# Output projection of a hybrid diffusion block: weight sums from the other tile pool, x reloaded inside the stage, and the seven products reordered

## The chip, the cores and the metric

The kernel runs on one core of a Trainium2 chip. The metric is the device time of one execution in microseconds (us). The median of three executions of the kernel before the change is 942.68 us (942.07 to 944.18).

## The reference, cut to what matters

One layer of a token mixer with a convolutional feed-forward part, for 512 tokens of width 1024, plus 256 context tokens that only give two start states. All data are float32.

```python
hx  = rms_norm(x) * (1 + sc1x) + sh1x            # sh, sc, g: silu(c) @ w_ada + b_ada
u, vs, q, r, ga, gb, k, v, lr = split(hx @ w_in)
a   = gelu(u) * spatial_gate(gelu(vs))
ob  = gated_linear_attention(q, k, v, lr) * silu(r)
merged = sigmoid(ga) * (a @ w_br_a) + sigmoid(gb) * (ob @ w_br_b)
x   = x + g1x * (merged @ w_o)                   # the output projection: w_o is 1024 x 1024
h2  = rms_norm(x) * (1 + sc2x) + sh2x
aa, val = split(h2 @ w_up)                       # 1024 -> 2 x 2816
x   = x + g2x * ((gelu(conv3x3(aa)) * val) @ w_down)
out = rms_norm(x)
```

## The kernel before

Tokens lie in tiles of 128 partitions for the residual stream (four token tiles `t`, each in two column halves `hf` of 512: `x1[t][hf]`), and transposed, feature on partition, as input of a matmul. Every float32 operand is split into a high and a low part (`wh`, `wl` for a weight, `mh`, `ml` for the merged activations, `h2h`, `h2l` for the second norm's output), and each product is done in three passes, high x high, high x low, low x high.

**The weight stream.** Weights come in blocks of 512 KB (two row groups of 128 by 512 columns). A list `loads` issues each block on SyncE's DMA queue into a tile `raw` (four buffers); a list `specs` splits it, ScalarE casting to `wh` (line L138), VectorE subtracting to get `wl` (L139). `weights(lead, ahead)` gives the next block to the matmuls, splits `lead` further ones and issues loads `ahead` of it.

**The output projection** is `strassen()`: the 1024 x 1024 by 1024 x 512 product done as seven half-size products instead of eight. A product `prod` has two weight blocks `j`, and for each of them two token halves by two row groups by three passes, which makes 24 matmuls of 128x512 (L443). The stages ga, gb and r of `w_in` use the same routine just before. `w_strassen` makes their weights: b11, b12, b21, b22 are the four quarters of the weight matrix. Some products want sums of quarters. They are built in four tiles `tt` (128x512 each, two for each `j`): b22 is loaded by SyncE (L199), b12 is added by a DMA with accumulation that GpSimd issues (L186, `add_rows`), this sum is split (L207 on ScalarE, L208 on VectorE; `t` in the list), then b11 is added by VectorE (L218; split as `t2`), and then b21 by a second accumulating DMA (split as `t4`). For `w_o` alone the sum b12 + b11 is made by an accumulating DMA into b12's raw tile (L192). In the order of their weights the seven products are a11, s3, s2, a12, s1, a22, s4. The left letter's accumulators are PSUM tiles `mm` and `gl`; ScalarE copies one into another where two products share a start (L452, L457, L461).

**After a product** is complete `wo_done` multiplies it by the gate g1 (L1447), adds it into `x1` (L1448) and has ScalarE sum the squares (L1449). When a token tile has both column halves, `norm2_tok` scales it (`xs`, L1422, after a reciprocal root, L479 and L480), and when two token tiles have it, `norm2_half` transposes them on the matmul engine (L1434, 16 matmuls of 128x128), ScalarE applies scale and shift (`h2f`, L1439), and VectorE splits the result into `h2h` and `h2l` (L1442, L1443). Tokens 256 to 511 are half 1, tokens 0 to 255 half 0. The feed-forward part starts with four groups of matmuls on 256 tokens of half 1 (L381, 96 matmuls of 128x256), then the same four for half 0 (L370), and from then on all 512 tokens.

**Around it.** `ada` work on the side computes the modulation vectors for later stages: weights `wa` are loaded into `late` tiles, VectorE accumulates them into `acc` (L1138), the sums are split (`acch`, `accl`; ScalarE L362, VectorE L363) and summed over partitions by two matmuls each (L1144, L1145).

**Pools and queues.** Two pools of 2 KB-per-partition tiles serve almost everything: `heap` with 44 slots and `late` with 27. A load into a reused slot waits for the last reader of the old tile. `tt`, the splits of `acc`, `xs` and `h2f` come from `heap`; `x1`, `br`, `os`, `wa` and `acc` come from `late`. Each engine works through its instructions in one fixed order, and SyncE's and GpSimd's DMA issues also stand in one order each, so an issue that waits holds those behind it. The order is made when the program is built, by a scheduler that goes by the order of the code, the dependencies and when slots come free; `tc.add_manual_dep` forces one instruction behind another.

## Time and profile before

| what | value |
|---|---|
| median of 3 executions | 942.68 us (942.07 to 944.18) |
| the profiled execution | 942.39 us, of which 940.7 us are the span from first to last instruction |
| TensorE (PE) busy | 908.0 us, 97% of the span |
| VectorE (DVE) busy | 761.5 us, 81% |
| ScalarE (ACT) busy | 477.6 us, 51% |
| GpSimd (POOL) busy | 62.1 us, 7% |
| mean granted TensorE clock | 0.986 |

Times in the views are microseconds from the span's start. A row of the timeline gives start, duration, engine, line, operation, output <- input, sizes, count, and in square brackets how long the engine was idle before it and what released it. A row of the table by stretches gives busy time and count for PE, PE's weight loads, DVE, ACT and POOL, the granted clock, the share of DMA capacity and GB/s. Matmuls overlap, so the time of one is read from start to start.

### The profile page before, as it was taken

How to read it: one execution, taken by the hardware profiler on the slowest of the kernel's cores; microseconds unless marked ns; L12 is line 12 of the kernel's file. 1: busy time of each engine (PE TensorE's matmuls, PEld its weight loads, DVE VectorE, ACT ScalarE, POOL GpSimd, SP SyncE). 2: the span in 40 equal slices, each digit the busy share in tenths (PEclk: the TensorE clock that was granted, in tenths of full speed). 3: DMA queues.
4: the chain of work that ended last, by engine and by line, in shares of the span. 5: the costliest groups of instructions: out<-in, count | busy, mean ns of one | idle time of the engine just before them, and what ended most of it. 6: DMA issues, size and time to landing. Idle time of an engine off the chain costs nothing.

```text
span 940.7 us, 12862 instructions
## 1 busy us (share of the span) xinstructions
PE 908.0 (97%) x4671; PEld 759.8 (81%) x4671; DVE 761.5 (81%) x1328; ACT 477.6 (51%) x855; POOL 62.1 (7%) x90
## 2 busy tenths in 40 slices
PE   6999999999999999999999798999999999999996
PEld 5776898988888888888888677988888888888885
DVE  5567759688589877877776779699999998999797
ACT  5136546557465547566552366434333333466574
POOL 3000000000000011112001010000000000122100
PEclk9999999999999999999999989999999999999998
DMA  9941411131079375988545275244444333499532
GB/s 274 331 127 26 132 46 46 46 112 52 17 243 328 106 186 123 288 260 205 178 136 125 57 167 157 66 124 135 125 118 129 111 113 96 106 244 240 135 108 90
DMA packets 125821, 134.27 MB, mean 143 GB/s; under 512 B 7178, under 2 KB 84310, under 8 KB 125758
## 3 DMA queue, kind: packets, MB, share of 16 engines
q1 hardware_dynamic: 115357, 116.80, 39.8%
q0 software_dynamic: 8672, 15.43, 9.9%
q10 hardware_dynamic: 1728, 1.22, 0.4%
q8 instruction: 37, 0.61, 0.3%
q14 instruction: 27, 0.21, 0.1%
HBM read 131.32 MB, written 2.10 MB: 142 GB/s over the span
## 4 chain that ended last, share of the span: by engine, by line
PE 57%; DVE 30%; issue 5%; ACT 4%; DMA 4%; ACTq 0%; SPq 0%; DVEq 0%; POOL 0%; POOLq 0%
PE mm L370 9%; DVE cacc L1484 9%; PE gl L443 7%; PE mm L396 6%; DVE wl L139 6%; PE gl L1586 6%; PE mm L443 5%; PE mm L1586 4%; PE gl L396 3%; PE gl L885 3%; PE mm L389 2%; DVE acc L1138 2%; PE mm L675 2%; ACT wh L138 1%; PE mm L381 1%
## 5 line engine op out<-in xcount | busy, mean ns | idle before, releaser
L138 ACT CAST wh<-raw 128x1024 fp32r<-128x1024 f32 x110 | 115.0, 1049 | 115.8 <-PE mm L370 70.3
L139 DVE TENSOR_TENSOR wl<-raw,wh 128x1024 fp32r<-128x1024 f32 x110 | 133.7, 1218 | 36.9 <-ACT wh L138 36.5
L370 PE MATMUL mm<-h2l,wh 128*128 128x512 f32 (+1 forms) x352 | 133.6, 379 | 0.0
L370 PE MATMUL mm<-h2h,wh 128*128 128x512 f32 (+1 forms) x352 | 133.6, 379 | 0.0
L370 PE MATMUL mm<-h2h,wl 128*128 128x512 f32 (+1 forms) x352 | 133.5, 379 | 0.0
L1484 DVE SCALAR_TENSOR_TENSOR cacc<-ca,ccol,cacc 128x441 f32<-128x441 f32 (+2 forms) x176 | 121.5, 693 | 3.5
L370 PEld LDWEIGHTS mm<-h2h,wh 128*128 128x128 f32 x352 | 66.2, 188 | 12.6
L370 PEld LDWEIGHTS mm<-h2h,wl 128*128 128x128 f32 x352 | 66.2, 188 | 12.5
L370 PEld LDWEIGHTS mm<-h2l,wh 128*128 128x128 f32 x352 | 66.2, 188 | 12.3
L1485 ACT ACTIVATE cacc<-cacc 128x512 f32<-128x512 f32 x22 | 13.9, 633 | 72.6 <-DVE cacc L1484 72.5
L1138 DVE SCALAR_TENSOR_TENSOR acc<-wa,cs,acc 128x512 f32<-128x512 f32 x64 | 46.0, 746 | 4.4 <-DMA wa<-in_w_ada_dram 3.8
L207 ACT CAST wh<-tt 128x512 fp32r<-128x512 f32 x48 | 28.0, 620 | 27.8 <-DMA tt<-in_w_in_dram 8.9
L370 PE MATMUL mm<-hxh,wh 128*128 128x512 f32 x104 | 41.7, 401 | 0.0
L370 PE MATMUL mm<-hxh,wl 128*128 128x512 f32 x104 | 41.0, 394 | 0.0
L370 PE MATMUL mm<-hxl,wh 128*128 128x512 f32 x104 | 40.7, 392 | 0.0
L208 DVE TENSOR_TENSOR wl<-tt,wh 128x512 fp32r<-128x512 f32 x48 | 31.1, 684 | 8.9 <-ACT wh L207 8.8
L1528 ACT CAST wh<-raw 128x1024 fp32r<-128x1024 f32 x22 | 23.0, 1052 | 18.2 <-DVE raw L1539 8.1
L186 POOL DMA_DIRECT2D tt<-in_w_in_dram x24 | 20.8, 1044 | 166.8 <-DVE xl L1237 72.2
L1529 DVE TENSOR_TENSOR wl<-raw,wh 128x1024 fp32r<-128x1024 f32 x22 | 26.8, 1216 | 4.4 <-ACT wh L1528 4.3
L443 PE MATMUL mm<-wh,hxh 128*128 128x512 f32 x72 | 28.0, 389 | 0.0
L443 PE MATMUL mm<-wl,hxh 128*128 128x512 f32 x72 | 28.0, 389 | 0.0
L443 PE MATMUL mm<-wh,hxl 128*128 128x512 f32 x72 | 28.0, 389 | 0.0
(521 smaller groups left out, 2394.9 us busy)
## 6 DMA issues: line engine op xcount, KB each, us to landing
raw<-in_w_in_dram SPq DMA_DIRECT2D x54, 512.0 KB, 5.0
wa<-in_w_ada_dram SPq DMA_DIRECT2D x96, 256.0 KB, 5.9
raw<-in_ffn_w_up_dram SPq DMA_DIRECT2D x44, 512.0 KB, 3.8
raw<-in_ffn_w_down_dram SPq DMA_DIRECT2D x22, 512.0 KB, 3.4
tt<-in_w_in_dram POOLq DMA_DIRECT2D x24, 256.0 KB, 7.5
raw<-in_w_br_a_dram SPq DMA_DIRECT2D x8, 512.0 KB, 4.7
raw<-in_w_br_b_dram SPq DMA_DIRECT2D x8, 512.0 KB
raw<-in_w_o_dram SPq DMA_DIRECT2D x8, 512.0 KB, 4.5
```

What stands on the lines that cost most here:

```text
L138: A.copy(wh, raw)
L139: V.tensor_tensor(wl, raw, wh.bitcast(F32), op=ALU.subtract)
L207: A.copy(wh[:, kk, :], tt[j][kk])
L208: V.tensor_tensor(wl[:, kk, :], tt[j][kk], wh[:, kk, :].bitcast(F32), op=ALU.subtract)
L370: T.matmul(ps, a[:, k, :], b[:, c0:c0 + n], start=(k == 0 and i == 0), stop=(k == KT - 1 and i == 2))
L396: T.matmul(ps, a, b[:, k % 2, :], start=(k == 0 and i == 0), stop=(k == KT - 1 and i == 2))
L443: T.matmul(ps[t], a, b[:, kk, :], start=(first and i == 0), stop=(j == 1 and kk == 1 and i == 2), skip_group_check=again)
L885: T.matmul(ps, p_, q_, start=(start and z == 0), stop=(stop and z == 2))
L1138: V.scalar_tensor_tensor(a_, w_, cs[:, k, 0:1], a_, op0=ALU.mult, op1=ALU.add)
L1484: V.scalar_tensor_tensor(o, a_[:, r0 + dy:r1 + dy, c0 + dx:c1 + dx], wcol(tap), o, op0=ALU.mult, op1=ALU.add)
L1529: V.tensor_tensor(wl, raw, wh.bitcast(F32), op=ALU.subtract)
L1586: T.matmul(ps, a[:, t * P:(t + 1) * P], w[b][:, j, c0:c0 + n], start=(first and i == 0), stop=(last and i == 2), skip_group_check=again)
```

## The change

Four things are changed, all but the last for `w_o` alone.

1. The tiles `tt` of `w_o` come from `late` instead of `heap`.
2. The eight loads of x into `x1` (256 KB each) are no longer issued ahead of the stages (L1410) but inside the output projection's first step, behind the last load of b12 (`behind`).
3. `low_first`: the weights come in the order b11, t, t2, b12, t4, b21, b22, and the products in the order a11, s3, s2, s1, a22, a12, s4. The loads of b21 and b22 move back in the list to match. Half 1 of the tokens is now complete after a22 with two products (a12 and s4) still to come; before, with one (s4).
4. The high and low parts of the `ada2` sums come from `late` instead of `heap`.

```diff
+    def behind(start, name):
+        for i in traced()[start:]:
+            tc.add_manual_dep(i, name, mybir.DependencyInfo(
+                mybir.DependencyClass.NoSync, mybir.DependencyReason.DATA), reason="behind")
...
-                tt[j] = [heap([P, 512], s="tt") for _ in range(2)]
+                tt[j] = [(late if low_first else heap)([P, 512], s="tt") for _ in range(2)]
...
         specs.extend([split_b11(j) for j in js] + [(lambda j=j: split_t(j)) for j in js] + [split_t2(j) for j in js] +
-                     [split_raw("b21", j) for j in js] + [split_raw("b12", j) for j in js] +
-                     [(lambda j=j: split_t(j)) for j in js] + [split_raw("b22", j) for j in js])
+                     (t1 + t4 + b21 if low_first else b21 + t1 + t4) + [split_raw("b22", j) for j in js])
...
-                      (4, [load_b12(j) for j in js]), (6, [load_raw("b21", 1, 0, j) for j in js]),
-                      (10, [load_raw("b22", 1, 1, j) for j in js])):
+                      (4, [load_b12(j) for j in js]),
+                      (10 if low_first else 6, [load_raw("b21", 1, 0, j) for j in js]),
+                      (12 if low_first else 10, [load_raw("b22", 1, 1, j) for j in js])):
...
-    w_strassen(w_o[0], 0, True)
+    w_strassen(w_o[0], 0, True, True)
...
-        prod(a, "a12", True)
-        for t in range(2):
-            done(0, t, a[t], 1.0)
+
+        def c11():
+            prod(a, "a12", True)
+            for t in range(2):
+                done(0, t, a[t], 1.0)
+
+        if not low_first:
+            c11()
         prod(c, "s1", True)
...
         prod(b, "a22", True)
         for t in range(2):
             done(0, 2 + t, b[t], 1.0)
+        if low_first:
+            c11()
         prod(c, "s4", True)
...
-            ah, al = split_act(a_, s="acc", eng=A.copy)
+            ah, al = split_act(a_, s="acc", eng=A.copy, lo_pool=late, hi_pool=late)
...
+    def x1_load():
+        start = len(traced())
...
+        behind(start, last_load["b12"])
...
-    strassen(lambda name, k, t: [z[:, k * P:(k + 1) * P] for z in mg[name, t]], wo_done, do)
+    def wo_step():
+        if not x1:
+            x1_load()
+        do()
+
+    strassen(lambda name, k, t: [z[:, k * P:(k + 1) * P] for z in mg[name, t]], wo_done, wo_step, True)
```

The order of the program on each engine moves at four places. In the rows, the last number of a name is the buffer's own number, and the new program's lines are shifted (L181 is L186, L199 is L205, L207 is L213, L443 is L451, L1434 is L1454, L222 is L228, L363 is L371).

On SyncE's queue before, in the output projection: raw 5182 and 5184 are b11 (j 0 and 1), 5478 and 5481 are b12, 5484 and 5508 are b21; `tt` 5190 and 5191 belong to j 0, 5466 and 5467 to j 1.

```order
L181 DMA raw_1071_5182<-in_w_o_dram 128x2x512
L181 DMA raw_1072_5184<-in_w_o_dram 128x2x512
L181 DMA raw_1157_5478<-in_w_o_dram 128x2x512
L199 DMA tt_1075_5190<-in_w_o_dram 128x512
L199 DMA tt_1076_5191<-in_w_o_dram 128x512
L181 DMA raw_1158_5481<-in_w_o_dram 128x2x512
L181 DMA raw_1159_5484<-in_w_o_dram 128x2x512
L199 DMA tt_1153_5466<-in_w_o_dram 128x512
L199 DMA tt_1154_5467<-in_w_o_dram 128x512
```

On the same queue now, far ahead, in the stage of gb (the `raw` tiles are quarters of `w_in`; `tt` 5450 and 5451 are j 1 of `w_o`; `tt` 4515 belongs to the stage of r):

```order
L186 DMA raw_919_4381<-in_w_in_dram 128x2x512
L205 DMA tt_1075_5190<-in_w_o_dram 128x512
L186 DMA raw_923_4402<-in_w_in_dram 128x2x512
L205 DMA tt_1076_5191<-in_w_o_dram 128x512
L205 DMA tt_1145_5450<-in_w_o_dram 128x512
L186 DMA raw_937_4475<-in_w_in_dram 128x2x512
L186 DMA raw_940_4493<-in_w_in_dram 128x2x512
L205 DMA tt_1146_5451<-in_w_o_dram 128x512
L205 DMA tt_943_4515<-in_w_in_dram 128x512
```

All four `tt` loads of `w_o` left the place behind the wait for a free raw tile, and stand 19 to 25 issues ahead of b11; on GpSimd's queue their four adds stand directly ahead of the four first adds of the stage of r. Where they were, the queue now has b11, b12, the eight loads of x, b21, b22.

On the matmul engine before, at the end of the projection (s4's last matmuls, then the transposes of half 1):

```order
L443 MATMUL gl_1180_5607<-wl_1196_5703,mh_1121_5414 128x512
L443 MATMUL gl_1180_5607<-wh_1195_5702,ml_1122_5415 128x512
L1434 MATMUL gl_1211_5764<-ident_76,xs_1204_5747 128x128
L1434 MATMUL gl_1213_5776<-ident_76,xs_1204_5747 128x128
L1434 MATMUL gl_1215_5788<-ident_76,xs_1205_5748 128x128
```

The same engine now (wh 5676 is the first of s4's two weight blocks):

```order
L451 MATMUL gl_1178_5605<-wh_1190_5676,mh_1121_5414 128x512
L1454 MATMUL gl_1203_5720<-ident_76,xs_1196_5703 128x128
L1454 MATMUL gl_1205_5732<-ident_76,xs_1196_5703 128x128
L451 MATMUL gl_1178_5605<-wl_1191_5677,mh_1121_5414 128x512
L451 MATMUL gl_1178_5605<-wh_1190_5676,ml_1122_5415 128x512
L1454 MATMUL gl_1203_5720<-ident_76,xs_1201_5716 128x128
```

The transposes of half 1 moved from behind s4 into its middle, after the tenth of its 24 matmuls.

On ScalarE before, around the copies L461 that give s1 and s4 their start value (the raw tiles cast are b12 + b11):

```order
L461 COPY gl_1179_5606<-gl_1163_5522 128x512
L138 CAST wh_1181_5612<-raw_1158_5481 128x1024
L461 COPY gl_1180_5607<-gl_1164_5523 128x512
L207 CAST wh_1183_5628<-tt_1075_5190 128x512
L207 CAST wh_1183_5628<-tt_1076_5191 128x512
```

ScalarE now (the same copies are L469; the casts of `tt` 5190 and 5191 here are `t4`, that is, after b21's add):

```order
L143 CAST wh_1171_5566<-raw_1150_5465 128x1024
L213 CAST wh_1174_5584<-tt_1075_5190 128x512
L213 CAST wh_1174_5584<-tt_1076_5191 128x512
L469 COPY gl_1177_5604<-gl_1161_5518 128x512
L469 COPY gl_1178_5605<-gl_1162_5519 128x512
```

The two casts that wait for b21's accumulating DMA now stand ahead of the copies, and s1, the next product, starts from those copies.

On VectorE before, much earlier, in the last quarter of branch a (L222 are the sums of two quarters for the stage of ga, accl 3741 the low part of an `ada2` sum):

```order
L1234 TENSOR_TENSOR hxl_141_525<-hv_782_3719,hxh_140_524 128x256
L363 TENSOR_TENSOR accl_786_3741<-acc_631_3047,acch_785_3740 128x512
L222 TENSOR_TENSOR raw_811_3829<-raw_811_3829,raw_777_3696 128x1024
L222 TENSOR_TENSOR raw_824_3887<-raw_824_3887,raw_778_3698 128x1024
L139 TENSOR_TENSOR wl_823_3884<-raw_777_3696,wh_822_3883 128x1024
```

VectorE now:

```order
L1249 TENSOR_TENSOR hxl_141_525<-hv_782_3719,hxh_140_524 128x256
L228 TENSOR_TENSOR raw_811_3829<-raw_811_3829,raw_777_3696 128x1024
L228 TENSOR_TENSOR raw_824_3887<-raw_824_3887,raw_778_3698 128x1024
L371 TENSOR_TENSOR accl_786_3741<-acc_631_3047,acch_785_3740 128x512
L144 TENSOR_TENSOR wl_823_3884<-raw_777_3696,wh_822_3883 128x1024
```

The low part of the `ada2` sum moved behind the two sums that wait for loads of `w_in`. SyncE's queue there has a `tt` load of the stage of ga (256 KB) put between the two raw loads 3829 and 3887.

More of the change, by code (lines that the diff above doesn't have):

```diff
@@ L128, in backbone_kernel @@
     xin = tok_load(x[0], 4, heap)
-    specs, loads = [], []
+    specs, loads, last_load = [], [], {}
     def raw_tile(kn, n):
@@ L169, in w_wide, with w_strassen @@
                 w_cols(w, hf * 512, 512, 2 * k, 2, scaled)
-    def w_strassen(w, c0, add_b12=False):
+    def w_strassen(w, c0, add_b12=False, low_first=False):
         base = len(specs)
@@ L181, in load @@
                 dma(raws[name, j], blk(kh, nh, j).rearrange("(k p) c -> p k c", p=P))
+                last_load[name] = traced()[-1].name
             return load
@@ L233, in w_strassen @@
         js = range(2)
+        b21, t1 = [split_raw("b21", j) for j in js], [split_raw("b12", j) for j in js]
+        t4 = [lambda j=j: split_t(j) for j in js]
         specs.extend([split_b11(j) for j in js] + [(lambda j=j: split_t(j)) for j in js] + [split_t2(j) for j in js] +
-                     [split_raw("b21", j) for j in js] + [split_raw("b12", j) for j in js] +
-                     [(lambda j=j: split_t(j)) for j in js] + [split_raw("b22", j) for j in js])
+                     (t1 + t4 + b21 if low_first else b21 + t1 + t4) + [split_raw("b22", j) for j in js])
         for o, fs in ((0, [load_raw("b11", 0, 0, j) for j in js]), (2, [load_t(j) for j in js]),
-                      (4, [load_b12(j) for j in js]), (6, [load_raw("b21", 1, 0, j) for j in js]),
-                      (10, [load_raw("b22", 1, 1, j) for j in js])):
+                      (4, [load_b12(j) for j in js]),
+                      (10 if low_first else 6, [load_raw("b21", 1, 0, j) for j in js]),
+                      (12 if low_first else 10, [load_raw("b22", 1, 1, j) for j in js])):
             loads.extend((base + o + j, fs[j]) for j in js)
@@ L431, in wide_kk, with strassen @@
         wide_half(1, [gl() for _ in range(4)], acts, done, step, 2, 6)
-    def strassen(acts, done, step):
+    def strassen(acts, done, step, low_first=False):
         def prod(ps, name, again):
@@ L1405, in backbone_kernel @@
     x1 = []
-    for t in range(4):
-        row = []
-        for hf in range(2):
-            t_ = late([P, 512], s="x1")
-            dma(t_, x[0, t * P:(t + 1) * P, hf * 512:(hf + 1) * 512])
-            row.append(t_)
-        x1.append(row)
+    def x1_load():
+        start = len(traced())
+        for t in range(4):
+            row = []
+            for hf in range(2):
+                t_ = late([P, 512], s="x1")
+                dma(t_, x[0, t * P:(t + 1) * P, hf * 512:(hf + 1) * 512])
+                row.append(t_)
+            x1.append(row)
+        behind(start, last_load["b12"])
     ss2 = const([P, 4, 2], "ss2")
```

## The prediction

> **What bounds the kernel now.** I read the table by stretches first, to see in which stage the matmul engine (PE) is not full, then the timeline of that stage on all engines, then PE's alone.
>
> ```profile
> 526.00:534.70 8.70, 8.70 (x42) 7.01 (x40) 8.21 (x14) 3.83 (x7) 0.00 (x0) 1.00 0.09 25
> 534.70:542.20 7.50, 0.25 (x2) 0.05 (x1) 1.58 (x4) 1.34 (x3) 1.78 (x2) 0.80 0.71 172
> 542.20:549.00 6.80, 6.50 (x13) 4.13 (x14) 5.50 (x8) 4.17 (x8) 2.54 (x3) 0.50 0.51 80
> 549.00:576.50 27.50, 27.45 (x120) 22.34 (x119) 23.04 (x32) 17.61 (x29) 1.86 (x3) 0.99 0.71 194
> 576.50:580.50 4.00, 0.83 (x4) 0.40 (x4) 4.00 (x12) 2.88 (x7) 0.00 (x0) 0.96 0.80 237
> 580.50:583.40 2.90, 2.88 (x14) 2.89 (x15) 2.90 (x11) 2.53 (x8) 0.00 (x0) 0.50 0.16 42
> 583.40:596.60 13.20, 13.20 (x112) 13.20 (x112) 10.04 (x33) 5.90 (x13) 0.00 (x0) 0.99 0.14 39
> 596.60:800.00 203.40, 203.40 (x945) 170.40 (x944) 182.64 (x264) 75.31 (x98) 0.00 (x0) 1.00 0.39 118
> ```
>
> The second number is PE's busy time, the fourth VectorE's, the third from the end PE's clock. From 596.6 to 800 PE is full, so whatever arrives earlier at 596.6 shortens the run by as much. Two holes lie ahead: 534.7 to 549 (idle, then half clock) and 576.5 to 583.4.
>
> ```profile
> 531.15 0.68 DVE L1370 TENSOR_TENSOR mf<-mf,mf 128x512 f32<-128x512 f32 x1
> 531.76 0.68 DVE L218 TENSOR_TENSOR tt<-tt,raw 128x512 f32<-128x512 f32 x1
> ...
> 532.50 0.38 SPq L181 DMA_DIRECT2D raw<-in_w_o_dram  x1
> ...
> 533.00 0.87 SPq L199 DMA_DIRECT2D tt<-in_w_o_dram  x2
> ...
> 537.38 1.78 POOL L186 DMA_DIRECT2D tt<-in_w_o_dram  x2 [29.06 <-DMA tt<-in_w_o_dram]
> 541.48 1.14 ACT L207 CAST wh<-tt 128x512 fp32r<-128x512 f32 x2 [5.32 <-DMA tt<-in_w_o_dram]
> ```
>
> This is the first hole's cause. SyncE's next raw load, b21, needs the raw tile that the add L218 reads, so it goes out at 532.50, and only then the tt tiles of j 1 at 533.00. They land, GpSimd adds b12 (537.38), that lands 4.1 us later, ScalarE casts at 541.48, and the second half of s3 can start.
>
> ```profile
> 525.96 0.48 PE L443 MATMUL mm<-wh,mh 128*128 128x512 f32 x1
> ...
> 534.51 0.39 PE L443 MATMUL mm<-wh,ml 128*128 128x512 f32 x1
> 542.15 0.79 PE L443 MATMUL mm<-wh,mh 128*128 128x512 f32 x1 [7.25 <-ACT wh L207]
> ...
> 549.53 0.39 PE L443 MATMUL gl<-wh,ml 128*128 128x512 f32 x1
> ...
> 576.06 0.39 PE L443 MATMUL gl<-wh,ml 128*128 128x512 f32 x1
> 578.40 0.83 PE L1434 MATMUL gl<-ident,xs 128*128 128x128 f32 x4 [1.95 <-DVE xs L1422]
> 580.51 2.82 PE L1434 MATMUL gl<-ident,xs 128*128 128x128 f32 x12 [1.28 <-DVE xs L1422]
> ...
> 590.03 1.47 PE L1434 MATMUL gl<-ident,xs 128*128 128x128 f32 x12
> 591.25 0.36 PE L381 MATMUL mm<-h2l,wh 128*128 128x256 f32 x1
> ...
> 596.48 0.28 PE L381 MATMUL mm<-h2h,wl 128*128 128x256 f32 x1
> 596.60 0.28 PE L370 MATMUL mm<-h2h,wh 128*128 128x256 f32 x1
> ```
>
> Between 549.53 and 576.06 lie 117 starts, so a 128x512 matmul costs 26.53/117 = 0.227 us; one of 128x256 costs 0.12 (596.60 − 596.48), a transpose 0.10 (12 from 590.03 to 591.25). Of the projection's 168 matmuls 36 have run when the idle begins (534.51 + 0.23 = 534.74); the other 132 are worth 29.9 and take until 576.3, 41.6 later: 11.7 lost, of it 7.25 idle and most of the rest half clock until about 549. The second hole is VectorE's: from 576.5 to 583.4 it is busy throughout, because the last product's outputs, their residual adds and the scaling `xs` stand in a row, and PE has nothing left but the transposes that wait for them.
>
> **The ceiling.** With no stall, from 525.96: the first 36 as they were, 8.8; 132 more, 29.9; 32 transposes of both halves, 3.3; 96 × 0.12 = 11.5; in all 53.5. First L370 at 579.5 instead of 596.6: at most 17.1.
>
> **The change, part by part.**
>
> *tt from the other pool.*
>
> ```profile
> 522.81 1.23 DVE L139 TENSOR_TENSOR wl<-raw,wh 128x1024 fp32r<-128x1024 f32 x1
> 523.95 0.69 DVE L1348 SCALAR_TENSOR_TENSOR ml<-mf,mh 128x512 fp32r<-128x512 f32 x1
> ```
>
> The four tt loads are issued in the stage of gb, some 100 us ahead, and their b12 adds soon behind them. What SyncE holds back until 532.50 is then not on s3's path. s3's second half needs VectorE's `wl` of the last tt at 534.74. Following VectorE's new row order from the L139 at 522.81, with 0.61 for a 128x512 operation (531.76 − 531.15) and 1.14 for 128x1024 (523.95 − 522.81), it ends at about 532.4. So the idle and the half clock behind it go: 11.7.
>
> *What is late next.* (a) The second half of s2 needs `wl` of t2 at 541.1 and gets it at 541.3: nothing. (b) On ScalarE the casts of t4 stand ahead of the copies from which s1 starts. They wait for b21's adds, issued when VectorE has split t2 (534.8 and 537.2) and landing 4.1 or somewhat more later: 541.3 to 543. Then a cast and a copy, 0.5 to 0.6 each: s1 starts at 543.6 instead of 542.9. I take 0.7; from 0 to 2.
>
> *Products reordered.* Half 1 is complete after a22, with 48 matmuls (10.9 us) left instead of 24 (5.4). Its chain (outputs multiplied, added, squared, root, `xs`) now runs beside a12. VectorE has little room: from 526.00 to 596.60 its work is 8.21 + 1.58 + 5.50 + 23.04 + 4.00 + 2.90 + 10.04 = 55.3, against PE's 53.5, so the two are level and VectorE sets the pace. By its new order `xs` of half 1 comes at 562.8 to 564.2; the first transpose stands behind s4's tenth matmul, at 562.2. That leaves two stalls, 0.7 and 0.6, and the hole at s4's end goes, because the first L381 finds its input. (c) For half 0, VectorE finishes the last split at about 583.5 while L370 begins to ask at 582; from 0 to 1.5, I take 1.0.
>
> First L370: 579.5 + 0.7 + 1.3 + 1.0 = 582.5 instead of 596.6, a gain of 14.1.
>
> *x reloaded late.*
>
> ```profile
> 498.49 34.39 SPq L181 DMA_DIRECT2D raw<-in_w_o_dram  x2
> ```
>
> The eight loads of 256 KB leave the stages of gb and r, where PE was full with them, and are issued behind b12's last load, the first of these two issues, after which SyncE had nothing to send for over 30 us. They are needed after s1, at about 550. Nothing either way. The adds of b12 + b11 (L192) are as before.
>
> *acc splits in the other pool, and what their slots move.* At 341 us:
>
> ```profile
> 334.21 0.38 SPq L181 DMA_DIRECT2D raw<-in_w_in_dram  x1
> ...
> 334.77 0.69 DVE L363 TENSOR_TENSOR accl<-acc,acch 128x512 fp32r<-128x512 f32 x1
> ...
> 339.40 1.23 DVE L222 TENSOR_TENSOR raw<-raw,raw 128x1024 f32<-128x1024 f32 x1 [1.57 <-DMA raw<-in_w_in_dram]
> ...
> 341.68 0.68 DVE L363 TENSOR_TENSOR accl<-acc,acch 128x512 fp32r<-128x512 f32 x1
> 341.70 0.39 PE L1145 MATMUL mm<-accl,ones_r 128*128 128x512 f32 x1
> ```
>
> The first accl was made at 334.77, long before 341.70 where PE reads it. Now it stands behind the second L222, which waited for the raw load issued at 334.21 and landed at 339.4 (5.2 us for 512 KB). Ready: 339.4 + 1.14 + 0.6 = 341.2, just in time; but a tt load of 256 KB now stands ahead of that raw, worth up to half of those 5.2. If the landing slips by 1.0, PE waits 0.5. The second accl, ready at 342.3 before, now follows two splits and three small operations: about 0.8 more. PE has no idle there, so a stall counts in full. I take 1.3; from 0 (the loads overlap) to 2.6.
>
> Sum: 14.1 − 1.3 = 12.8. Against the profiled execution's own 942.39 (0.29 under the median of 942.68) that is 929.6.
>
> **The clock.** My sum has no clock term, since the new stalls are a third of those before 578.40 and 580.51. Those two, 1.95 and 1.28 with 0.83 of work between, were followed by 2.9 us at half clock (the row 580.50), so short gaps can cost; the rival below has that. The Trainium skill (TensorE: Matmul & The Clock Gate, "What's actually happening") has the half rate come after an idle window of about 3.4 us; by that rule neither those gaps nor the new ones would cost anything, and the trace disagrees where two follow one another.
>
> **The rivals.**
>
> *VectorE's row stalls on the accumulating DMAs* (0.13). If b21's adds land later than 543, the t4 splits and all behind them on VectorE slip, and at 55.3 of work there is no slack to make it up. Against it: 4.1 us from issue to use at 537.38. For it: four adds in 6 us, while x and b21 also load. 4.5 more would give first L370 at 587: 934.
>
> *The clock drops in s4* (0.10). If the stalls before the transposes count as those of 578.40 and 580.51, some 3 to 6 us at half clock follow, 1.5 to 3 lost: 931 to 932.6.
>
> *The change doesn't do what it says* (0.02): tt is late for another reason than the queue. Against it stand 532.50 and 533.00, back to back. Then only the second hole goes: 929.6 + 11.7 = 941.3.
>
> *Slower, by one queue* (0.03). On GpSimd the four adds of w_o stand ahead of the first adds of the stage of r, and the last of them waits for a tt load that SyncE issues only behind two raw loads.
>
> ```profile
> 425.71 1.76 POOL L186 DMA_DIRECT2D tt<-in_w_in_dram  x2 [14.97 <-DMA tt<-in_w_in_dram]
> ...
> 435.80 1.29 DVE L208 TENSOR_TENSOR wl<-tt,wh 128x512 fp32r<-128x512 f32 x2
> ...
> 436.26 0.39 PE L443 MATMUL mm<-wh,hxh 128*128 128x512 f32 x1
> ```
>
> r's s3, which uses that split, begins 24 × 0.227 = 5.4 after r's first matmul at 436.26, at 441.7, so the split done at 437.1 has 4.6 to spare. The delay I see is one landing and one issue, 1 to 2.5: hidden. To end slower it would have to exceed 4.6 + 12.8 = 17.4.
>
> **How the numbers follow.** My forecast, 927 to 932 for the sum with its ends, has 0.68; 0.04 lies below 927, where the stalls I count don't occur (floor 942.4 − 17.1 = 925.3). Measurement of this kernel can tell 0.2%, 1.9 us, from no change. Faster by more has 0.68 + 0.04 + 0.13 + 0.10 = 0.95, which I put at 0.94 for what I have not seen; same 0.03, the case of 941.3 and mixtures; slower 0.03. The range 926.0 to 934.5 takes in the clock rival and most of VectorE's, and leaves out less than 2 in 10.
>
> **What the profile of the changed kernel would show.** Right: no PE row of the projection waits for a cast of tt by more than 1 us between s3 and s1; the clock stays at 1.00 there; transposes run between s4's matmuls; first L370 13 to 15 us earlier against the projection's start; VectorE over 90% busy up to it; about a microsecond of PE idle at the `ada2` matmuls near 342. Wrong: several us of PE waiting on the splits of t4 or on `xs`, half clock in s4, or a new wait in the stages ga to r, which my count has at nothing.

## The result, and the profile after

The changed kernel takes 935.19 us (median of 10 runs, 932.55 to 942.67), the kernel before 943.00 in the same series (10 runs, 941.28 to 944.91). The ratio is 0.9925, with a 95% interval of 0.990 to 0.995. The gain is 7.8 us where 12.8 was forecast, and the time lies just above the range given. The profiled execution took 936.04 us, 6.35 less than the one of before; its span is 934.3.

The first fence is the timeline of TensorE in the changed kernel, at the places that divide the execution. The lines of the code have moved: L443 is now L451, L370 L378, L381 L389, L1422 L1442, L1434 L1454, L1586 L1611.

```profile
186.31 0.51 PE L900 MATMUL gl<-st,qh 128*128 128x256 f32 x2 [0.80 <-DVE mc L826]
...
345.42 0.50 PE L1159 MATMUL mm<-acch,ones_r 128*128 128x512 f32 x1 [1.40 <-ACT acch L370]
...
442.24 0.50 PE L451 MATMUL mm<-wl,hxh 128*128 128x512 f32 x1 [1.47 <-DVE wl L144]
...
529.18 0.48 PE L451 MATMUL mm<-wh,mh 128*128 128x512 f32 x1
...
568.57 0.44 PE L1454 MATMUL gl<-ident,xs 128*128 128x128 f32 x2 [3.12 <-DVE xs L1442]
...
588.56 0.28 PE L378 MATMUL mm<-h2h,wh 128*128 128x256 f32 x1
...
830.89 0.47 PE L1611 MATMUL mm<-wh,sh 128*128 128x512 f32 x1 [1.39 <-DVE cacc L1511]
...
926.14 0.28 PE L1611 MATMUL mm<-wh,ol 128*128 128x128 f32 x1
```

Four waits are new, at 345, 442, 568 and 831, and the two holes of before are gone. The rows of before that answer to the first and the last are these; the other two (525.96 and 596.60) stand in the prediction.

```profile
186.22 0.50 PE L885 MATMUL gl<-st,qh 128*128 128x256 f32 x2 [0.80 <-DVE mc L811]
...
932.50 0.28 PE L1586 MATMUL mm<-wh,ol 128*128 128x128 f32 x1
```

So the time can be read in three stretches. A runs from the row at 186 to the projection's first matmul, B from there to the first matmul on half 0's columns (L370, now L378), C from there to the last matmul. What lies before and behind differs by 0.1 between the two.

| stretch | before | after | gain | forecast gain |
|---|---|---|---|---|
| A, stages up to the projection | 339.74 | 342.87 | −3.1 | −1.3 |
| B, the projection | 70.64 | 59.38 | 11.3 | 14.1 |
| C, the feed-forward part | 335.90 | 337.58 | −1.7 | 0 |
| sum | 746.28 | 739.83 | 6.5 | 12.8 |

All three stretches came out worse than forecast, by 1.8, 2.8 and 1.7. The table by stretches of the projection shows its part of it (busy time and count of PE, its weight loads, DVE, ACT, POOL; then the granted clock, the share of DMA capacity and GB/s):

```profile
529.20:538.00 8.80, 8.80 (x43) 7.14 (x41) 8.80 (x15) 4.74 (x10) 0.00 (x0) 1.00 0.01 2
538.00:546.60 8.60, 8.39 (x38) 6.61 (x37) 8.56 (x14) 7.00 (x13) 4.13 (x6) 1.00 0.76 176
546.60:552.00 5.40, 5.40 (x24) 4.48 (x25) 2.51 (x5) 1.98 (x3) 0.29 (x1) 1.00 1.05 276
552.00:557.50 5.50, 5.50 (x26) 4.57 (x25) 4.34 (x6) 2.53 (x3) 0.00 (x0) 1.00 0.30 89
557.50:563.00 5.50, 5.50 (x26) 4.55 (x25) 5.50 (x9) 3.65 (x7) 0.00 (x0) 1.00 0.72 207
563.00:568.50 5.50, 2.45 (x11) 1.69 (x9) 5.50 (x12) 5.03 (x10) 0.00 (x0) 1.00 0.55 162
568.50:570.00 1.50, 1.44 (x11) 1.12 (x11) 1.50 (x5) 0.82 (x3) 0.00 (x0) 1.00 1.15 307
570.00:572.00 2.00, 2.00 (x8) 1.61 (x6) 2.00 (x4) 1.52 (x3) 0.00 (x0) 0.51 0.71 176
572.00:574.00 2.00, 2.00 (x9) 1.61 (x9) 1.90 (x6) 1.63 (x4) 0.00 (x0) 0.63 0.61 175
574.00:588.50 14.50, 14.50 (x121) 14.32 (x120) 12.29 (x36) 8.17 (x19) 0.00 (x0) 1.00 0.29 85
```

Until 563 TensorE is busy at a clock of 1.00, but for the 0.21 us that s1 waits for ScalarE's copy. VectorE is full except between 546.6 and 557.5, where 4.05 us are missing, and in the first of these two rows the DMA share is 1.05. From 557.5 VectorE is full again and cannot make them up, so `xs` is late and TensorE waits 3.12 us. Some 1.5 us after it has started again its clock drops to one half. A row's clock is the mean of stretches at 0.5 and at 1, so the two rows with 0.51 and 0.63 hold 2 × 2 × 0.49 + 2 × 2 × 0.37 = 3.4 us at half speed, and 1.7 us are lost. What holds VectorE up stands in the timeline of GpSimd, ScalarE and VectorE:

```profile
538.42 0.87 POOL L192 DMA_DIRECT2D tt<-in_w_o_dram  x1 [29.82 <-DVE wl L214]
541.13 0.85 POOL L192 DMA_DIRECT2D tt<-in_w_o_dram  x1 [1.85 <-ACT es L465]
543.29 0.84 POOL L192 DMA_DIRECT2D tt<-in_w_o_dram  x1 [1.31 <-DVE wl L214]
545.03 0.85 POOL L192 DMA_DIRECT2D tt<-in_w_o_dram  x1 [0.90 <-DVE wl L214]
...
549.69 0.62 ACT L213 CAST wh<-tt 128x512 fp32r<-128x512 f32 x1 [2.68 <-DMA tt<-in_w_o_dram]
552.51 0.62 ACT L213 CAST wh<-tt 128x512 fp32r<-128x512 f32 x1 [1.24 <-DMA tt<-in_w_o_dram]
...
550.34 0.69 DVE L214 TENSOR_TENSOR wl<-tt,wh 128x512 fp32r<-128x512 f32 x1 [1.93 <-ACT wh L213]
553.16 0.69 DVE L214 TENSOR_TENSOR wl<-tt,wh 128x512 fp32r<-128x512 f32 x1 [2.12 <-ACT wh L213]
```

The adds of b21 for the second weight block go out at 543.29 and 545.03, when VectorE has split t2. Their sums are used 6.4 and 7.5 us later, where 4.1 was seen in the kernel before.

### The profile page after: what moved, and what is told of

The parts are those of the page before. It is cut to its first block, busy times and chain, and to the rows that moved or that the text cites. A ratio compares the mean times of both kernels' runs of the same rounds, so it can differ in the third digit from the quotient of the medians.

```text
span 934.3 us, 12863 instructions
## 1 busy us (share of the span) xinstructions
PE 904.9 (97%) x4671; PEld 757.5 (81%) x4671; DVE 760.8 (81%) x1328; ACT 477.7 (51%) x855; POOL 62.0 (7%) x90
## 4 chain that ended last, share of the span: by engine, by line
PE 75%; DVE 11%; DMA 7%; ACT 3%; issue 3%; SPq 0%; ACTq 0%; POOL 0%; DVEq 0%; POOLq 0%
PE mm L378 32%; PE mm L404 9%; PE gl L1611 6%; PE mm L1611 4%; DMA tt<-in_w_in_dram 4%; PE gl L451 3%; PE gl L900 3%; PE mm L397 3%; PE mm L451 2%; PE gl L404 2%; PE mm L690 2%; DVE wl L144 1%; DMA raw<-in_w_in_dram 1%; PE mm L389 1%; PE mm L1004 1%
## 5 line engine op out<-in xcount | busy, mean ns | idle before, releaser
L144 DVE TENSOR_TENSOR wl<-raw,wh 128x1024 fp32r<-128x1024 f32 x110 | 134.1, 1222 | 27.1 <-ACT wh L143 24.4
L378 PE MATMUL mm<-h2l,wh 128*128 128x512 f32 (+1 forms) x352 | 133.6, 379 | 0.0
L378 PE MATMUL mm<-h2h,wh 128*128 128x512 f32 (+1 forms) x352 | 133.6, 379 | 0.0
L378 PE MATMUL mm<-h2h,wl 128*128 128x512 f32 (+1 forms) x352 | 133.5, 379 | 0.0
L378 PEld LDWEIGHTS mm<-h2h,wl 128*128 128x128 f32 x352 | 66.2, 188 | 12.6
L378 PEld LDWEIGHTS mm<-h2l,wh 128*128 128x128 f32 x352 | 66.2, 188 | 12.5
L378 PEld LDWEIGHTS mm<-h2h,wh 128*128 128x128 f32 x352 | 66.2, 188 | 12.3
L378 PE MATMUL mm<-hxh,wh 128*128 128x512 f32 x104 | 41.7, 401 | 0.0
L378 PE MATMUL mm<-hxh,wl 128*128 128x512 f32 x104 | 40.9, 394 | 0.0
L378 PE MATMUL mm<-hxl,wh 128*128 128x512 f32 x104 | 40.7, 392 | 0.0
L213 ACT CAST wh<-tt 128x512 fp32r<-128x512 f32 x48 | 28.5, 623 | 22.9 <-DMA tt<-in_w_in_dram 11.3
L451 PE MATMUL mm<-wl,hxh 128*128 128x512 f32 x72 | 28.1, 391 | 1.5 <-DVE wl L144 1.5
L451 PE MATMUL mm<-wh,hxh 128*128 128x512 f32 x72 | 28.0, 389 | 0.0
L451 PE MATMUL mm<-wh,hxl 128*128 128x512 f32 x72 | 28.0, 389 | 0.0
```

Of the source, the lines that this page charges most:

```text
L144: V.tensor_tensor(wl, raw, wh.bitcast(F32), op=ALU.subtract)
L213: A.copy(wh[:, kk, :], tt[j][kk])
L378: T.matmul(ps, a[:, k, :], b[:, c0:c0 + n], start=(k == 0 and i == 0), stop=(k == KT - 1 and i == 2))
L451: T.matmul(ps[t], a, b[:, kk, :], start=(first and i == 0), stop=(j == 1 and kk == 1 and i == 2), skip_group_check=again)
```

## The experiments

Each line of the table is one kernel: the median with its number of runs, the ratio to the kernel before in the same series with its interval, and A, B and C of its profiled execution, read from the same four rows of its trace. A profile is one execution. A varies by 1.8 us among the four kernels that differ only behind it (after, after_again, no_t4_add, hold_b22), because the waits at 345 and 442 come and go. In undo_acc, t4_own, pools_only and x_early a wait inside A is also followed by half clock, for 3.4 us (6.8 in undo_acc), which costs half of that. The part ahead of the row at 186 runs from 184.8 to 188.0. So the medians decide on small effects, and B and C show where.

| kernel | us (runs) | ratio | A | B | C |
|---|---|---|---|---|---|
| before | 941.8 to 943.0 | 1 | 339.74 | 70.64 | 335.90 |
| after | 935.19 (10) | 0.990 to 0.995 | 342.87 | 59.38 | 337.58 |
| after_again | 935.22 (6) | 0.9905 to 0.9942 | 343.39 | 57.64 | 336.96 |
| undo_acc | 932.44 (6) | 0.9878 to 0.9913 | 345.75 | 57.68 | 335.79 |
| tt_behind_r | 933.03 (6) | 0.9878 to 0.9922 | 341.12 | 57.89 | 336.99 |
| no_t4_add | 929.84 (4) | 0.9852 to 0.9884 | 341.64 | 54.62 | 336.79 |
| hold_b22 | 930.69 (4) | 0.9869 to 0.9896 | 342.68 | 56.63 | 337.27 |
| t4_own | 931.55 (5) | 0.9867 to 0.9906 | 347.34 | 54.61 | 336.97 |
| two_fixes | 929.09 (4) | 0.9853 to 0.9883 | 339.36 | 59.44 | 335.72 |
| three_fixes | 927.93 (4) | 0.9829 to 0.9873 | 341.06 | 56.33 | 335.66 |
| all_three | 925.80 (5) | 0.9809 to 0.9843 | 340.21 | 54.54 | 335.74 |
| pools_only | 939.44 (7) | 0.9960 to 0.9993 | 344.26 | 62.46 | 337.03 |
| order_only | 938.93 (12) | 0.9958 to 0.9978 | 339.39 | 67.36 | 335.74 |
| x_early | 934.44 (6) | 0.9900 to 0.9930 | 344.96 | 60.74 | 337.04 |
| acc_only | 946.92 (6) | 1.0034 to 1.0062 | 341.24 | 71.22 | 337.06 |

**The changed kernel again**, to see which waits recur.

> The changed kernel once more, for a second profile. Theory (late arrivals): the stalls of the first profile come from fixed orders and from transfers that land late, so all of them recur: about 1.4 us of PE idle before an ada2 matmul near 345, about 1.5 on a split of r's weights near 442, 2 to 4 on xs near 568 with half clock behind it, 1 to 2 on the convolution's sum near 831. Rival (chance): they are accidents of one execution, and at least two of the four are under 0.3 us this time. Time 933 to 938 either way.

935.22, the same. Its profiled execution has a slightly shorter wait at the same place:

```profile
567.34 0.44 PE L1454 MATMUL gl<-ident,xs 128*128 128x128 f32 x2 [2.83 <-DVE xs L1442]
...
568.00:570.00 2.00, 2.00 (x14) 1.66 (x12) 2.00 (x4) 1.68 (x3) 0.00 (x0) 1.00 0.96 240
570.00:572.00 2.00, 2.00 (x12) 1.44 (x11) 2.00 (x6) 1.26 (x4) 0.00 (x0) 1.00 0.27 74
```

After 2.83 us of idle time the clock stays at 1.00, after 3.12 it fell. B is 1.74 shorter for it: 0.29 is the wait, most of the rest the clock. The other three waits recur, at 345 with 1.88, at 441 with only 0.49, and at 828 with 1.42; a wait of 0.78 on `accl` at 341 is added.

**b21's add left out of t4**, which takes away the adds, their traffic and the wait for them together.

```diff
-                add_rows(j, 1, 0)
+                if not low_first:
+                    add_rows(j, 1, 0)
```

> The changed kernel without the four accumulating DMAs that add b21 into tt in w_o (the sum t4 then lacks b21; all else is computed). Theory (late arrivals): VectorE stands idle for 1.9 and 2.1 us near 550 because the casts of t4 wait for these adds, which share the DMA engines with the loads of b21 and b22; without them xs of half 1 comes about 4 us earlier, the PE stall of 3.1 near 568 and the half clock behind it go: 4 to 5.5 us less than the changed kernel, about 930.5. Rival (VectorE's load sets the pace of the projection, 55 us of work against 53.5): it has no slack to win back, xs comes at most 1 us earlier: about 934.5.

929.84, that is 5.4 less than the changed kernel. No wait on `xs` is left, the clock is at 1.00, and B is 54.62. That is what the projection takes when TensorE never waits for more than 0.21 us; my ceiling had it at 53.5.

**Is it the traffic or the chain?** The adds could land late because they share the DMA with raw loads, or the chain of split, issue, add and cast could be too long by itself. Holding b22's two raw loads back changes the traffic alone.

```diff
                 last_load[name] = traced()[-1].name
+                if low_first and name + str(j) in ("b220", "b221"):
...
+                    tc.add_manual_dep(traced()[-1], last_load["t4"], mybir.DependencyInfo(
+                        mybir.DependencyClass.Sync, mybir.DependencyReason.DATA), reason="hold")
...
                 add_rows(j, 1, 0)
+                if low_first and j == 1:
+                    last_load["t4"] = traced()[-1].name
```

> The two raw loads of b22 (512 KB each) wait until the last of the four adds of b21 into tt has landed; nothing else differs from the changed kernel, and the order on every engine is the same. Theory, the adds land late because they share the DMA with raw loads issued at 542.5: the last two adds land about 5 us after their issue instead of 6.4 and 7.5, so VectorE's two idle stretches of 1.93 and 2.12 us before the last splits of t4 shrink to less than 2 us together, TensorE's stall on xs shrinks below 2 us, and the median falls by 2 to 4 to 931 to 933. Rival, the chain itself is too long (a split must have read tt before the add may start, and an add takes what it takes): no change, 934.5 to 936. A second rival, b22 now comes too late for s4: TensorE waits on wh of b22 and the median is above 936.

930.69, and the intervals do not overlap with the changed kernel's. These are ScalarE, VectorE and TensorE of that run, with b21's last two adds issued at 541.69 and 543.42:

```profile
548.11 0.62 ACT L217 CAST wh<-tt 128x512 fp32r<-128x512 f32 x1 [2.71 <-DMA tt<-in_w_o_dram]
549.59 0.61 ACT L217 CAST wh<-tt 128x512 fp32r<-128x512 f32 x1
...
548.76 0.69 DVE L218 TENSOR_TENSOR wl<-tt,wh 128x512 fp32r<-128x512 f32 x1 [1.95 <-ACT wh L217]
550.24 0.69 DVE L218 TENSOR_TENSOR wl<-tt,wh 128x512 fp32r<-128x512 f32 x1 [0.78 <-ACT wh L217]
...
565.64 0.44 PE L1460 MATMUL gl<-ident,xs 128*128 128x128 f32 x2 [1.80 <-DVE xs L1448]
```

The theory holds for the last add and fails for the one before: used 6.2 instead of 7.5 after its issue, and 6.4 as before. I had expected about 5 for both. VectorE's idle time falls by 1.3, TensorE's wait by 1.3, and since 1.80 is followed by no half clock, B falls by 2.75. So b22's loads explain 1.3 of the wait, and without these 1.3 the clock did not fall. The other 1.8 is not told apart further here: b21's own load still runs beside the adds. Of the 4.65 between the two profiled executions B is 2.75; 1.4 lies ahead of the row at 186, which the edit does not touch, so the median's 4.5 may overstate what holding b22 is worth.

**t4 in tiles of its own** takes the chain away instead: b22 is loaded a second time, and b12, b11 and b21 are added by DMA while SyncE has nothing else to send.

```diff
+        def load_t4(j):
+            start = len(traced())
+            t4s[j] = [late([P, 512], s="tt4") for _ in range(2)]
+            for kk in range(2):
+                dma(t4s[j][kk], blk(1, 1, j)[kk * P:(kk + 1) * P, :])
+            for kh, nh in ((0, 1), (0, 0), (1, 0)):
+                for kk in range(2):
+                    G.dma_start(t4s[j][kk], blk(kh, nh, j)[kk * P:(kk + 1) * P, :], accum_op=ALU.add)
+            behind(start, last_load["b12"])
...
-                add_rows(j, 1, 0)
+                if low_first:
+                    tt[j] = t4s[j]
+                else:
+                    add_rows(j, 1, 0)
```

> The sum t4 gets four tiles of its own, loaded with b22 and added up by twelve DMAs (b12, b11, b21) behind b12's last load, 4 MB instead of 1 MB, all issued before about 530; nothing of it waits for a split any more. Theory: VectorE's two idle stretches before the splits of t4 go, xs comes about 4 us earlier, TensorE's stall of 3 us there and the half clock behind it go, and the median is 929 to 931, as when b21's add was left out (929.8). Rival, VectorE's row is too full to use it: 933 to 935. Second rival, the extra 3 MB delay b12's add or the loads of x: a new wait before s1, above 935.

931.55, a little above the theory's 929 to 931 and below both rivals. B is 54.61, the same as with the add left out, so VectorE's row is not too full and the 3 MB more are hidden in the projection. Its profiled execution, the slowest of the five, loses in A: 1.85 at 345, and 2.25 on `wl` (L144) at 444.22 with half clock behind it. Why the wait at 444 is longer than the 1.47 of the changed kernel is not told apart; with the two remedies below it is gone (all_three, A 340.21).

**The stage of r**: w_o's tt loads behind r's last raw load.

```diff
+                start = len(traced())
                 for kk in range(2):
                     dma(tt[j][kk], blk(1, 1, j)[kk * P:(kk + 1) * P, :])
+                if low_first:
+                    behind(start, last_load["b22"])
```

> The changed kernel with the four tt loads of w_o made to stand behind the last load of r's b22, so that they and their adds run some 30 us later; nothing else moves on any engine. Theory (late arrivals): in the changed kernel these loads and adds (2 MB) share the DMA engines with r's raw loads and delay their landing from 433.5 to 439.8, which makes the stall near 442 (1.5 us): it goes, 1.2 to 1.8 us less than the changed kernel, about 933.5, and w_o's s3 is as early as before. Rival: the stall near 442 comes from GpSimd's queue or from VectorE's order and stays: about 935.

933.03: the wait at 442 is gone, 2.2 less than the changed kernel, though the two intervals overlap. VectorE's sums of two quarters (L228, here L231) wait for raw loads of r's stage, in the changed kernel (first two) and here (last two):

```profile
436.17 1.23 DVE L228 TENSOR_TENSOR raw<-raw,raw 128x1024 f32<-128x1024 f32 x1 [6.88 <-DMA raw<-in_w_in_dram]
439.82 1.23 DVE L228 TENSOR_TENSOR raw<-raw,raw 128x1024 f32<-128x1024 f32 x1 [2.42 <-DMA raw<-in_w_in_dram]
```

```profile
431.92 1.23 DVE L231 TENSOR_TENSOR raw<-raw,raw 128x1024 f32<-128x1024 f32 x1 [1.82 <-DMA raw<-in_w_in_dram]
435.05 1.23 DVE L231 TENSOR_TENSOR raw<-raw,raw 128x1024 f32<-128x1024 f32 x1 [1.91 <-DMA raw<-in_w_in_dram]
```

From 410 to 440 us the DMA moves 7.38 MB in the kernel before, 8.34 in the changed one and 6.71 here. The raw loads land 4.3 and 4.8 us earlier when tt does not stand among them. The loads and their adds moved together, so the two are not told apart.

**acc's splits** back in heap (undo_acc, the edit shown), and the same part of the change alone, the same line turned round in the kernel before (acc_only).

```diff
-            ah, al = split_act(a_, s="acc", eng=A.copy, lo_pool=late, hi_pool=late)
+            ah, al = split_act(a_, s="acc", eng=A.copy)
```

> The changed kernel with the high and low parts of the ada2 sums back in the heap pool; its other three parts stay. Theory (late arrivals): this part of the change alone costs the stall near 345 (1.4 us) and, by the order that it gives to the last feed-forward group, the stalls near 821 and 831 (1.7 together): both go, 2.5 to 3 us less than the changed kernel, about 932. Rival (VectorE's load is what bounds the ends): the stall near 831 stays, since VectorE is full there in any order, and only 1.4 goes: about 934.

932.44, and as expected the waits at 345 and 831 go. But two others come in its profiled execution, 1.70 and 0.76 at 418, where w_o's tt loads now stand ahead of two raw loads, and 6.8 us at half clock behind them. That is why its A, 345.75, is 2.9 longer than the changed kernel's. The median gains 2.8 all the same.

> The kernel before with one change, the splits of acc in late. Theory, this alone costs what undoing it gained (2.8): TensorE waits near 342 to 346 for acch and near 838 for cacc, 944 to 946.5 against 942 to 943. Rival, its cost arises only together with the moved tt loads, and alone it is hidden: 942 to 943.5.

946.92, so this part alone costs 4.5 us (3.2 to 5.8). The rows of that kernel:

```profile
344.64 0.50 PE L1144 MATMUL mm<-acch,ones_r 128*128 128x512 f32 x1 [1.60 <-ACT acch L362]
...
839.63 0.47 PE L1586 MATMUL mm<-wh,sh 128*128 128x512 f32 x1 [1.38 <-DVE cacc L1486]
```

Its profiled execution was the fastest of the six (944.79), and these two, 2.98 together, more than cover its 2.4. What the others lose beyond that no trace shows. The wait at 831 is a matter of order: `cacc` is made as far along VectorE's row as before, but TensorE comes to it after two matmuls of the other accumulator instead of eight, which is 6 × 0.227 = 1.4 earlier. It waits 1.39 there, where it waited 0.37 before. C is 335.7 to 335.9 in every kernel with acc's splits in heap, and 336.8 to 337.6 in every one with them in late.

**The two remedies together**, then with the third.

> The splits of acc are back in heap, and the tt loads of w_o are held behind r's last raw load. Theory, the two losses are separate and add up: no TensorE wait at 345, 418, 442 and 831 us, the stall on xs stays; 935.2 - 2.8 - 2.2 = 930.2 (929 to 931.5). Rival, the gains overlap or turn into a new wait in the stages of gb and r: 932 to 933.5.

929.09, and none of the waits of A is left (A 339.36, as before the change). The wait on `xs` is 3.25, followed by half clock: B 59.44.

> acc's splits in heap, w_o's tt loads behind r's last raw load, b22's raw loads held until b21's adds have landed. Theory, the three losses are separate: 935.2 - 2.8 - 2.2 - 4.5 = 925.7, and with TensorE's stall on xs under 3.05 us (the longest that was followed by no half clock so far; 3.12, 3.25 and 3.31 were) the clock stays at 1.00: 924 to 927. Rival, VectorE's row is full and the stall on xs stays near 3 us: 927.5 to 929.5, no better than the two fixes alone (929.1).

927.93 (925.50 to 931.02), in the rival's range, and its interval overlaps with that of the two fixes. The mechanism is the theory's all the same: the wait on `xs` is 1.54 and the clock in the projection 1.00. The profiled execution was the slowest of the four, with 2.7 us of idle time at 32 us and half clock behind it, and 1.44 at 345, where `accl` came behind a raw load that landed late although acc's splits were in heap.

> t4 with tiles of its own (as in the run that had them alone), acc's splits in heap, w_o's tt loads behind r's last raw load. Theory: the time is the sum of three stretches that the parts set separately. Up to the projection's first matmul 339.5 us from the mark at 185, as in the run with the two fixes; the projection 54.6, as with t4's own tiles; from the first matmul on half 0's columns to the last one 335.7, as in every run with acc in heap; 8.2 behind it and 1.8 around the span: 185 + 339.5 + 54.6 + 335.7 + 8.2 + 1.8 = 924.8 (923.5 to 926.5), with no TensorE wait on xs and the clock at 1.00 in the projection. Rival, the 3 MB that t4's own tiles add cost what they save, as the run with them alone (931.6) suggests: a new wait in r's or the projection's stage, 927.5 to 930.

925.80, a ratio of 0.9826 (0.9809 to 0.9843), better than both kernels of the case. These are all of TensorE's waits of 0.2 us or more behind 230 us:

```profile
416.56 0.50 PE L470 MATMUL mm<-wl,hxh 128*128 128x512 f32 x1 [0.38 <-DVE wl L144]
...
542.55 0.50 PE L470 MATMUL gl<-wh,mh 128*128 128x512 f32 x1 [0.21 <-ACT gl L488]
...
821.65 0.47 PE L1630 MATMUL mm<-wh,sh 128*128 128x512 f32 x1 [0.24 <-DVE cacc L1530]
```

The stretches add up, within 1 us of 924.8.

**The change in two halves**: without the new order, and the new order alone.

```diff
-                tt[j] = [(late if low_first else heap)([P, 512], s="tt") for _ in range(2)]
+                tt[j] = [(late if tt_late else heap)([P, 512], s="tt") for _ in range(2)]
...
-    w_strassen(w_o[0], 0, True, True)
+    w_strassen(w_o[0], 0, True, False, True)
...
-    strassen(lambda name, k, t: [z[:, k * P:(k + 1) * P] for z in mg[name, t]], wo_done, wo_step, True)
+    strassen(lambda name, k, t: [z[:, k * P:(k + 1) * P] for z in mg[name, t]], wo_done, wo_step)
```

The fourth argument is the new order, now off, and the fifth, `tt_late`, keeps tt in late.

> The change without the new order: tt and the splits of acc in late, x reloaded inside the stage, but weights and products in the order of before. Theory: the first hole (11.7 us) goes, the second one stays as it was, the losses at 345, 442 and 831 us stay (about 4 us together); 943.0 - 11.7 + 4 = 935.3 (934 to 937), so that the new order by itself brings nothing that shows in the changed kernel. Rival, by my prediction's sum the order is worth 17.1 - 11.7 - 3.0 = 2.4: 937 to 939.

939.44, not the 935.3 of my theory, and a little above the rival's 937 to 939. The first hole does not go for nothing: here s1 waits for the split of b12 + b11 (two waits, 1.66 together), and the second hole is longer than it was. In A the wait of 1.85 at 345 is followed by 3.4 us at half clock.

```profile
550.76 0.50 PE L451 MATMUL mm<-wh,mh 128*128 128x512 f32 x1 [0.90 <-ACT wh L143]
...
552.02 0.50 PE L451 MATMUL mm<-wl,mh 128*128 128x512 f32 x1 [0.76 <-DVE wl L144]
...
574.47 3.61 PE L1454 MATMUL gl<-ident,xs 128*128 128x128 f32 x16 [3.31 <-DVE xs L1442]
```

```diff
-                tt[j] = [(late if low_first else heap)([P, 512], s="tt") for _ in range(2)]
+                tt[j] = [heap([P, 512], s="tt") for _ in range(2)]
...
-            ah, al = split_act(a_, s="acc", eng=A.copy, lo_pool=late, hi_pool=late)
+            ah, al = split_act(a_, s="acc", eng=A.copy)
...
-        behind(start, last_load["b12"])
...
+    x1_load()
```

> The new order of weights and products alone: tt and acc's splits in heap, x loaded early, as before the change. Theory, the first hole stays, since tt waits for the same heap slots and raw tiles, and b21's adds come as late as they did; the order is worth what it was worth on top of the pools (939.4 - 935.2 = 4.2), 937 to 941. Rival, behind the first hole the adds of b21 land so late that VectorE's row slips as well and a stall on xs with half clock takes the whole gain: 942 to 946.

938.93, as the theory had it. The first hole stays, the second is gone, with no wait on `xs`, and a wait of 1.21 on a copy for s1 comes at 555.7:

```profile
539.97 0.79 PE L451 MATMUL mm<-wh,mh 128*128 128x512 f32 x1 [6.82 <-ACT wh L213]
```

So the order is worth 3.5 alone and 4.2 on top of the pools (by the medians of two series; 4.9 by the two ratios), and the pools with the reload 2.5 alone, in which the costs of acc and of r's stage are counted.

**x loaded early**, everything else as changed: `x1_load()` ahead of the stages instead of behind b12.

> The changed kernel, but with the eight loads of x issued ahead of the stages, as before the change; they take late slots, so that two of the four tt loads of w_o now come in the stage of w_br_b. Theory, x reloaded late was worth something, since raw loads, tt loads and x share the DMA in the stage of r: with x back there TensorE's wait for wl near 441 grows to 2 us or more, 936 to 939. Rival, my prediction's (x early or late is worth nothing): 934.5 to 936, or less, since two of the tt loads leave the stage of r.

934.44, so my theory fell: the interval overlaps with that of the changed kernel. The run changes two things at once, since two of w_o's tt loads also move to a later stage, and together they make no measurable difference. The wait at 441 is gone in its profiled execution, the slowest of the six, but neither is shown to be the reason: TensorE begins r there at 440.54 instead of 437.66, 3.9 us later counted from the row at 186, after waits of 1.61 and 1.85 near 345 and a half clock, while r's raw block is split only 0.4 sooner by the same count.

## Why the prediction was right or wrong

**The first hole: right.** No row of s3 waits for a cast of tt, and the clock stays at 1.00 there. That tt stood behind b21 on SyncE's queue was its cause; with tt left in heap (order_only) SyncE issues the last two tt loads at 531.25, right behind a raw load that had waited, and the hole is there again.

**The second hole: the mechanism right, the size off.** The order was taken to be worth 17.1 − 11.7 − 3.0 = 2.4 and is worth 3.5 to 4.9.

**VectorE's row: the step that failed most, 2.8 us.** For b21's adds I took the first two issues and 4.1 us, and asked only whether ScalarE's copies for s1 would be late. They were not: s1 starts 0.21 late, where I took 0.7. But the adds of the second block go out 4.9 and 3.9 us after those, and take 6.4 and 7.5. My times of `xs` (562.8 to 564.2) assumed sums that had landed. On before's time scale (3.2 earlier) the first transpose ran at 565.3, a wait of 3.12 instead of 0.7 and 0.6. The rival that named this, VectorE's row on the accumulating DMAs, had 0.13, and the clock's rival 0.10. Both happened at once, the second because of the first, and the sum had put the clock at nothing. Of B's 59.38, 54.5 is what the projection takes without these (all_three), 3.1 the wait, 1.7 the half clock. The ceiling of 53.5 was thus 1.0 too low, and the 1.0 that I took for half 0's splits did not come at all; that the two cancel is luck.

**The stage of r: a wrong step, 1.5 us.** I counted w_o's adds ahead of r's on GpSimd and found 4.6 to spare. The loss came from the loads: four of 256 KB, with their four adds, among r's raw loads. VectorE's split of r's own raw block, which I had not followed, was made at 440.96 instead of 434.67, with TensorE 1.4 later than before; it had some 3.5 us to spare.

**acc's splits: nearly the right sum at 341, by luck, for the wait is another.** Of 1.3 forecast 1.40 came. The first `accl` was just in time, as worked out; the wait is for the second `acch` on ScalarE, which stands there behind two other casts and a copy. ScalarE had been idle for 3.48 us before the first of these casts, waiting for an `xl` that stands on VectorE behind the two sums that wait for raw loads. In other executions the wait was up to 1.9, with 0.4 to 1.6 for `accl` besides in some.

**C: a term that was missing, 1.7 us.** I followed acc's slots only at 341. The same splits are made again in the feed-forward part, the scheduler orders the last group another way, and TensorE asks for `cacc` 1.4 earlier. About 1.2 of the 1.7 is shown by all kernels with acc in late; 0.35 more is a wait on a copy at 821, which the second execution (after_again) does not have.

**x: nothing either way**, as forecast: the loads are issued from 502.14 and VectorE's first add into `x` comes at 557.84. The run x_early agrees in its time but moves two tt loads as well.

The signs that I gave for being wrong were the ones that came: TensorE waiting on `xs`, half clock in s4, and a new wait between ga and r.

## What to carry to other kernels

When a wait is removed, follow every accumulating add to the engine that reads its sum, the last of them above all, and price it with the traffic that will run beside it, not with the landing time of an idle stretch. A buffer that moves to another pool moves every later use of both pools: go through all places where the same line runs, not only the next one. Where an engine's row is full, a wait in it arrives at its end (1.3 us less idle time of VectorE was 1.3 less waiting of TensorE in hold_b22); take the producer out of the row (sums made by idle DMA time gave back all 4.8 us of the projection here) before ordering consumers more finely.

## What the runs showed of the hardware

**The clock changes on a fixed grid of 3.41 us, and what counts is how much of one grid step TensorE stands idle.** In the kernel before, the granted clock, by the trace's own record of it, changes at 10.18, 20.42, 27.25, 539.25, 549.49, 580.21, 583.62 and 935.19 us. The differences are 3, 2, 150, 3, 9, 1 and 103 times 3.413, and in each of the fifteen traces all changes lie on such a grid. So the time at half speed is 3.4 us or a multiple: 3.4 after single waits of 3.12, 3.25 and 3.31 before the transposes, 6.8 after 3.47, and 10.2 behind the hole of 7.25 in the kernel before. The 2.9 us that my prediction read behind the second hole are 3.4 by this record. Here are steps of the grid in the changed kernel (first three rows), in tt_behind_r (next two) and in pools_only (last two):

```profile
563.23:566.64 3.41, 2.22 (x10) 1.50 (x8) 3.41 (x7) 3.38 (x8) 0.00 (x0) 1.00 0.25 70
566.64:570.06 3.42, 1.50 (x11) 1.18 (x11) 3.42 (x9) 2.29 (x5) 0.00 (x0) 1.00 1.09 309
570.06:573.47 3.41, 3.41 (x13) 2.72 (x11) 3.31 (x7) 2.66 (x7) 0.00 (x0) 0.50 0.59 151
...
565.67:569.08 3.41, 1.56 (x11) 1.25 (x12) 3.41 (x9) 2.29 (x5) 0.00 (x0) 1.00 1.04 299
569.08:572.49 3.41, 3.41 (x18) 2.59 (x18) 3.41 (x8) 2.67 (x7) 0.00 (x0) 1.00 0.58 165
...
343.04:346.46 3.42, 1.57 (x7) 0.99 (x6) 2.25 (x3) 2.19 (x4) 0.00 (x0) 1.00 0.64 193
346.46:349.87 3.41, 3.41 (x10) 2.62 (x9) 1.29 (x2) 1.62 (x3) 0.00 (x0) 0.50 0.72 237
```

The wait of 3.12 lies across two steps, with 1.92 us of idle time in the second, and the next step runs at one half. The wait of 3.05 in tt_behind_r leaves 1.85 in the second step, and the clock stays at 1.00. A wait of only 1.85 that lies in one step is enough in pools_only, while one of 1.88 in after_again (at 345) that leaves 1.71 in a step is not. In the fifteen traces, of the steps that ran at 1.00, all 30 with more than 1.9 us of idle time were followed by half clock, none with less than 1.75 was, and the 12 between went either way. So whether a wait of 2 to 3 us costs 1.7 us more depends on where the grid lies in that execution. The Trainium skill (TensorE: Matmul & The Clock Gate, "What's actually happening") has the clock set by windows of 3413 ns that run freely, and the runs agree with that length. The rule that my prediction quotes from the Trainium skill, half rate after an idle window, they do not bear out: 1.92 of 3.41 us idle was enough here.

**An accumulating DMA that GpSimd issues takes about twice the engines' time per byte of a load that SyncE issues.** No run has the one without the other, so the adding and the queue are not told apart. From 536 to 556 us of the changed kernel, by queue (packets, MB, share of 16 engines), software being GpSimd's adds and hardware SyncE's loads:

```profile
q0 software_dynamic: 576, 1.05, 32.1%
q1 hardware_dynamic: 1088, 2.10, 30.9%
```

32.1/1.05 is 30.6% a MB, 30.9/2.10 is 14.7%: a factor of 2.1. From 410 to 440 us it was 47.6% for 2.55 MB against 56.8% for 5.77 MB, a factor of 1.9. Four adds of 256 KB thus weigh like 2 MB of loads, which my count of transfers had not in it.
